# The first feed-forward's begun blocks: squares from token rows on ScalarE, the second input normalised on GpSimd, blocks begun in pairs, and an order of its own on each engine

## The chip, the cores and the metric

The kernel runs on one core of a Trainium2 chip. The core has a matrix engine (TensorE, in the profile PE), three engines for elementwise work (VectorE or DVE, ScalarE or ACT, GpSimd or POOL) and an engine that only issues transfers (SyncE or SP). Each engine works through a queue of its own in order; engines wait for each other by semaphores. The metric is the device time of one execution in microseconds (us), lower is better. Before the change it is 2115.48 us, the median of three runs.

## The reference

One encoder layer works on two inputs, `x_prompt` and `x_sample`, of 512 tokens by 1024 channels each. It is a half-step SwiGLU feed-forward, a mixing block (attention and an mLSTM side by side), a second half-step feed-forward and a last norm. Everything is float32. The change touches the first feed-forward:

```python
def rms_norm(x, g):
    y = xf * lax.rsqrt(jnp.mean(xf * xf, axis=-1, keepdims=True) + EPS)
    return (y * g.astype(jnp.float32)).astype(x.dtype)

def swiglu(x, w_gate, w_up, w_down):
    return (jax.nn.silu(x @ w_gate) * (x @ w_up)) @ w_down

x = x + 0.5 * swiglu(rms_norm(x, ffn1_norm), ffn1_w_gate, ffn1_w_up, ffn1_w_down)
```

`w_gate` and `w_up` are 1024 x 2816, that is 22 blocks of 128 columns each.

## The kernel before

**Products.** A float32 factor is split into a high part (ScalarE copies it into a shorter format) and a low part (VectorE subtracts the high part from it); `w_pair` does both for a weight block. A product is then three matmuls per 128 channels: high by high, high by low, low by high. `product` runs over 4 groups of 128 channels, so one product is 12 matmuls of 128 x 128 x 512.

**Seven products for eight.** The kernel treats the two inputs and the gate and up weights as a 2 x 2 block problem and multiplies it by a scheme with seven products (B11, B21, T2, T1, T3, B22, T4) in place of eight. The left factors are sums and differences of weight halves, the right factors `xc[...]` are sums and differences of the halves of the two normalised inputs (`x0l`, `x0u` of the first, `x1l`, `x1u` of the second). B11 and B21 need the first input only and give the first input's gate product: B11 is the lower half of its channels, B21 the upper half.

**Begun blocks.** Before the second input is ready TensorE can do B11 and B21 of a block. The kernel begins 12 of the 22 blocks in this way (`AHEAD[0]` is 12): for each, it evicts the sum after B11 (ScalarE, to SBUF), adds B21, takes the Silu of the whole, and stores both results in DRAM buffers `kept[j]`. Later, `up.rest` takes the blocks up again in the order 0, 12, 1, 13, ...: for begun blocks it loads `kept[j]`, for the others it does all seven products. The first product that isn't begun work is T2 of block 0; in the profile it is the first matmul group that writes `pss`.

**Raw blocks.** The norm's scale isn't known at the start. So the first six blocks (`RAW` is 6) multiply the raw input times the gain, split by `split_x`, and their results are multiplied by the scale `R[0]` afterwards (`raw_end`: two multiplies on VectorE, a Silu on ScalarE, two stores). Blocks 6 to 11 use the normalised input.

**The scale.** The inputs stand channel-major (`x_t`). `squares` squares 1024 columns at a time on ScalarE and adds them up on VectorE; `norm` adds the rest, sums over channels by transposes and a reduction (`col_sums`), takes the root in 11 small VectorE steps (`rstd_cols`), spreads the result over the partitions by transposes, and copies it to `R[s]`. `normed` multiplies the input by gain and scale, eight VectorE instructions of 512 columns for each input (L1247).

**What sets the order.** A scheduler orders the instructions of each engine, except where `pin` (`tc.keep_in_program_order`) keeps them as written. The matmuls of blocks, their weight loads (`up.left`) and the evictions of raw blocks aren't pinned. The weight loads go through four buffers (`wr`), the split weights through four others (`w8`). All loads and stores of this stretch are issued by SP, in SP's order; the small loads of the gains (`mix_gains`, L621 to L623) are issued by GpSimd.

```python
def raw_lower(j):                                  # L1251
    X = begun[j] = [PO() if j % 4 == 3 else MM(), held_rows[j % 4]]
    product(X[0], W[j][B11], xr[0], True)
    nc.scalar.activation(X[1], X[0], AF.Copy)
...
def raw_next(j):
    W.append(gu_left_a(raw2[0]) if j == 2 else up.left(j))
    raw_lower(j)
    raw_upper(j)

def ahead(j):
    W.append(up.left(j))
    up.begin(j, W[j])
```

Lines that the profile names: L249 and L250 are the high and low part of a weight block, L1229 and L1230 those of the raw input, L1282 and L1283 those of half an input (2048 columns), L290 is every matmul of `product`, L1254 the eviction of a raw block, L1234 and L1236 the squares and their sum, L1262 and L1263 the multiplies of `raw_end`, L1161 a square with its accumulator in a later stage, L892 and L1449 GpSimd's multiplies and adds in later stages.

Of the kernel before, what the change touches and what calls it, by code (L numbers as in the profile page):

```python
# [8 lines left out]
F32 = mybir.dt.float32  # L9
# [17 lines left out]
def encoder(ctx, tc, I, outs):  # L27
# [97 lines left out]
    nc.sync.dma_start(g1, I["ffn1_norm"])  # L125


# [5 lines left out]
    warm = cpool.tile([P, 1], F32, name="warm")  # L133
    nc.scalar.activation(warm, ones[:, 0:1], AF.Silu)
# [112 lines left out]

    def w_pair(t, src, pin=lambda i: i):
        pin(nc.scalar.activation(t[:, 0], src, AF.Copy))  # L249
        pin(V_.tensor_tensor(t[:, 1], src, f(t[:, 0]), op=ALU.subtract))  # L250
# [13 lines left out]
    def gu_left_b(rg, ru, ring, left):  # L264
# [5 lines left out]
        V_.tensor_tensor(a, u0, u1, op=ALU.add)  # L270
        V_.tensor_tensor(u0, g0, u0, op=ALU.subtract)
        V_.tensor_tensor(g0, a, g0, op=ALU.subtract)
        V_.tensor_tensor(g1_, g1_, g0, op=ALU.subtract)
        wb = w8_tile()
        w_pair(wb, halves(rg))
        left.update({T2_: part(wb, 0), B22: part(wb, 1)})

        def more():
            wd = [v(ring.wd(F32R)) for _ in range(2)]
            split(a, *wd)  # L280
            wc = w8_tile()
            w_pair(wc, halves(ru))
            left.update({T1: wd, T3: part(wc, 0), T4: part(wc, 1)})
# [95 lines left out]
    class Up:  # L379
# [33 lines left out]
        def rest(self, raw, at=None, hook=None):  # L413
            ring, ORDER = self.ring, self.order

            def resume(j):
                got = ring.v(), ring.h()
                for t, d in zip(got, self.kept.pop(j)):
                    nc.sync.dma_start(t[:, 0], d)
                return got  # L420

            left = {}
            gu_left_b(*raw, ring, left)()
            raw = self.fetch(ORDER[1])
            got = resume(ORDER[0])
# [192 lines left out]
    def mix_gains():  # L618
        pin = tc.keep_in_program_order
        for t, n in ((gm, "mix_norm"), (g2, "ffn2_norm")):  # L620
            pin(nc.gpsimd.dma_start(t, I[n][0].rearrange("(k p) -> p k", p=P)))  # L621
        pin(nc.gpsimd.dma_start(gbias, I["mlstm_gate_bias"].rearrange("a c -> (a c)").partition_broadcast(P)))
        pin(nc.gpsimd.dma_start(hn, I["mlstm_head_norm"][0].rearrange("(k p) -> p k", p=P)))  # L623
# [568 lines left out]
    def load_x(s, a, b):  # L1192
        nc.sync.dma_start(x_t[s][:, a:b, :], x_in[s][:, a:b, :])
# [3 lines left out]
    def load_half(j, a):  # L1197
        nc.sync.dma_start(half(first_w[j], a), half(up.v[0][j], a))

    load_half(0, 0)  # L1200
    load_x(0, 0, 1)
# [7 lines left out]
    raw2 = up.fetch(2, (0,))  # L1209
    for k in range(0, KD, 2):  # L1210
        load_x(1, k, k + 2)

    rings = up.ring
    stat = rings.x.rows[:3]
    held_rows = [t[:, i] for t in rings.x.rows[3:] for i in range(2)]
# [3 lines left out]
    W = [{}, {}]  # L1219

    def first_left(j, a):
        if a == 0:
            W[j]["t"] = w8_tile()
        w_pair(W[j]["t"][:, :, a], half(first_w[j], a))
        W[j][(B11, B21)[a]] = part(W[j]["t"], a)

    def split_x(k):
        t, kk, g, x = xr[k // HK_], k % HK_, g1[:, k:k + 1], x_t[0][:, k, :]
        nc.scalar.activation(t[:, 0, kk, :], x, AF.Copy, scale=g)  # L1229
        V_.scalar_tensor_tensor(t[:, 1, kk, :], x, g, f(t[:, 0, kk, :]), op0=ALU.mult, op1=ALU.subtract)  # L1230

    def squares(s, i):
        sq = stat[0] if i == 0 else stat[1 + i % 2]
        pin(nc.scalar.activation(sq, x_t[s][:, 2 * i:2 * i + 2, :], AF.Square))  # L1234
        if i:
            pin(V_.tensor_tensor(stat[0], stat[0], sq, op=ALU.add))  # L1236

    def norm(s):
        acc = stat[0][:, 0]
        pin(V_.tensor_tensor(acc, acc, stat[0][:, 1], op=ALU.add))  # L1240
        r = rstd_cols(col_sums(acc, pin=pin), 4, D, pin)
        pin(nc.scalar.activation(R[s], bcast_psum(r), AF.Copy))

    def normed(s):
        for k in range(KD):
            x = x_t[s][:, k, :]
            pin(V_.scalar_tensor_tensor(x, x, g1[:, k:k + 1], R[s], op0=ALU.mult, op1=ALU.mult))  # L1247
# [3 lines left out]
    def raw_lower(j):  # L1251
        X = begun[j] = [PO() if j % 4 == 3 else MM(), held_rows[j % 4]]
        product(X[0], W[j][B11], xr[0], True)
        nc.scalar.activation(X[1], X[0], AF.Copy)  # L1254

    def raw_upper(j):
        product(begun[j][0], W[j][B21], xr[1], False)

    def raw_end(j):
        X, v1 = begun.pop(j)  # L1260
        g0 = gate_rows()
        pin(V_.tensor_tensor(v1, v1, R[0], op=ALU.mult))  # L1262
        pin(V_.tensor_tensor(g0, X, R[0], op=ALU.mult))  # L1263
        pin(nc.scalar.activation(g0, g0, AF.Silu))
        up.kept[j] = kept[j]
        for t, d in zip((v1, g0), kept[j]):
            nc.sync.dma_start(d, t)

    def raw_next(j):
        W.append(gu_left_a(raw2[0]) if j == 2 else up.left(j))  # L1270
        raw_lower(j)
        raw_upper(j)

    def ahead(j):
        W.append(up.left(j))
        up.begin(j, W[j])
# [4 lines left out]
    def put_all(t, src):  # L1281
        pin(nc.scalar.activation(t[:, 0], src, AF.Copy))  # L1282
        pin(V_.tensor_tensor(t[:, 1], src, f(t[:, 0]), op=ALU.subtract))  # L1283
# [4 lines left out]
    raw_lower(0)  # L1288
    first_left(1, 0)
    first_left(0, 1)  # L1290
    for k in range(HK_, KD):
        split_x(k)
        if k % 2:
            squares(0, k // 2 - 2)
    raw_lower(1)
    raw_upper(0)
    first_left(1, 1)
    raw_upper(1)
    squares(0, 2)
    squares(0, 3)  # L1300
    norm(0)
    raw_next(2)
    raw_end(0)
    raw_end(1)
    raw_next(3)
    raw_end(2)
    normed(0)
    raw_next(4)
    raw_end(3)
    xc[B11], xc[B21] = xc_tile(), xc_tile()  # L1310
    for i, t in zip((B11, B21), halves(0)):
        put_all(xc[i], t)
    raw_next(5)
    raw_end(4)
    for i in range(4):
        squares(1, i)
    norm(1)
# [262 lines left out]
```

## Time and profile before

| | |
|---|---|
| median of 3 runs | 2115.48 us (2114.89 to 2115.61) |
| profiled execution: time, span | 2114.9 us, 2113.1 us |
| TensorE busy | 2067.0 us, 98% of the span |
| VectorE, ScalarE, GpSimd busy | 75%, 44%, 5% |
| granted TensorE clock, mean | 0.993 |
| memory traffic | 173 GB/s mean |

A profile row of an instruction group gives line, engine, operation, output<-inputs by the program's names with buffer numbers left out, size and count; then busy time and mean ns of one; then the engine's idle time just before the group and what ended it. A timeline row begins with the start and the length in us and ends with the idle time before it in brackets. A row of a stretch gives the window, its length, the busy us of PE, PEld (weight loading), DVE, ACT and POOL with their counts, the granted clock, the busy share of the 16 DMA engines and GB/s. A row of transfers gives the count, the KB of each and the median us from issue to landing.

### The profile page before, as it was taken

The page shows a single profiled execution, that of the slowest core. Times are in us where ns is not written, and L with a number is a line of the kernel's source. Part 1 is how long each engine was busy: PE and PEld are TensorE (multiplying, and loading weights), DVE is VectorE, ACT ScalarE, POOL GpSimd, SP SyncE. Part 2 cuts the span into 40 slices and gives each one's busy share as a digit, 9 for nine tenths or more (in the row PEclk, how much of TensorE's full clock was granted, in tenths as well). Part 3 has the DMA queues.
Part 4 walks back from the last instruction along what each step waited for, and adds up shares of the span by engine and source line. Part 5 has one row for each costly group of instructions (what it writes and reads, how often), then busy time and mean ns, then how long its engine had stood idle before and what let it go on. Part 6 is the DMA issues. An engine that isn't in the chain of part 4 may idle for free. (4 is left out here: it accounts for less than half of the span.)

```text
span 2113.1 us, 26149 instructions
## 1 busy us (share of the span) xinstructions
PE 2067.0 (98%) x9424; PEld 1689.1 (80%) x9424; DVE 1575.7 (75%) x2568; ACT 939.7 (44%) x1559; POOL 100.6 (5%) x105
## 2 busy tenths in 40 slices
PE   8899999999999999999999999999999999999997
PEld 6688888888888777878887787788788888888886
DVE  7978788786786796574649865764887877776687
ACT  6534344442225566463436555544543434343224
POOL 0000000001000110000101101010000000000002
PEclk9999999999999999999999999999999999999999
DMA  7445564699764222232341222344546544369753
GB/s 249 152 168 180 179 229 166 241 361 360 250 229 144 75 71 73 81 116 85 119 160 56 75 92 79 130 156 166 167 156 222 179 170 179 140 247 400 280 208 140
DMA packets 140625, 365.96 MB, mean 173 GB/s; under 512 B 13808, under 2 KB 13824, under 8 KB 139472
## 3 DMA queue, kind: packets, MB, share of 16 engines
q1 hardware_dynamic: 139648, 362.50, 48.4%
q0 software_dynamic: 560, 1.26, 0.2%
q8 instruction: 74, 1.21, 0.2%
q10 hardware_dynamic: 288, 0.52, 0.1%
q14 instruction: 55, 0.45, 0.1%
HBM read 258.82 MB, written 105.41 MB: 172 GB/s over the span
## 5 line engine op out<-in xcount | busy, mean ns | idle before, releaser
L290 PE MATMUL pss<-xc,w 128*128 128x512 f32 x1584 | 378.4, 390 | 0.7 <-DVE t L320 0.7
L290 PEld LDWEIGHTS pss<-xc,w 128*128 128x128 f32 x1584 | 297.3, 188 | 63.3 <-DVE t L320 1.4
L698 PE MATMUL mm<-xh,w 128*128 128x512 f32 x896 | 293.4, 397 | 0.9 <-DVE w L212 0.9
L290 PE MATMUL mm<-xc,w 128*128 128x512 f32 x1032 | 252.9, 397 | 18.0 <-DVE w L250 8.3
L249 ACT ACTIVATE w<-wr 128x1024 fp32r<-128x1024 f32 (+1 forms) x134 | 139.8, 1047 | 254.0 <-PE pst L290 134.3
L290 PEld LDWEIGHTS mm<-xc,w 128*128 128x128 f32 x1032 | 195.1, 191 | 64.0 <-DVE w L250 8.8
L250 DVE TENSOR_TENSOR w<-wr,w 128x1024 fp32r<-128x1024 f32 (+1 forms) x134 | 161.4, 1206 | 82.2 <-ACT w L249 81.5
L212 DVE TENSOR_TENSOR w<-wr,w 128x1024 fp32r<-128x1024 f32 (+1 forms) x112 | 135.4, 1210 | 116.2 <-ACT w L211 111.3
L698 PEld LDWEIGHTS mm<-xh,w 128*128 128x128 f32 x896 | 167.8, 189 | 33.4 <-DVE w L212 1.3
L542 PE MATMUL mm<-w,rt 128*128 128x512 f32 x792 | 185.3, 390 | 0.0
L698 PE MATMUL mm<-xl,w 128*128 128x512 f32 x448 | 177.4, 396 | 0.0
L542 PEld LDWEIGHTS mm<-w,rt 128*128 128x128 f32 x792 | 148.6, 188 | 30.7
L211 ACT ACTIVATE w<-wr 128x1024 fp32r<-128x1024 f32 (+1 forms) x112 | 114.6, 1030 | 109.8 <-PE pso L1127 35.0
L290 PE MATMUL pst<-xc,f 128*128 128x512 f32 x528 | 127.3, 390 | 0.0
L290 PE MATMUL pst<-xc,w 128*128 128x512 f32 x528 | 127.2, 390 | 0.0
L290 PEld LDWEIGHTS pst<-xc,w 128*128 128x128 f32 x528 | 99.0, 188 | 20.9 <-ACT t L323 0.5
L290 PEld LDWEIGHTS pst<-xc,f 128*128 128x128 f32 x528 | 99.2, 188 | 20.5
L602 ACT ACTIVATE w<-t 128x512 fp32r<-128x512 f32 x82 | 51.6, 632 | 121.9 <-PE pst L542 63.6
L602 ACT ACTIVATE w<-wr 128x512 fp32r<-128x512 f32 x72 | 44.7, 631 | 128.1 <-PE pso L542 62.0
L698 PEld LDWEIGHTS mm<-xl,w 128*128 128x128 f32 x448 | 84.6, 189 | 16.1
L542 PE MATMUL pss<-w,rt 128*128 128x512 f32 x396 | 94.4, 390 | 0.1
L542 PE MATMUL pst<-w,rt 128*128 128x512 f32 x396 | 94.0, 389 | 0.0
(344 smaller groups left out, 3506.2 us busy)
## 6 DMA issues: line engine op xcount, KB each, us to landing
rt<-rbuf SPq DMA_DIRECT2D x154, 512.0 KB, 6.0
rbuf<-t SPq DMA_DIRECT2D x72, 512.0 KB, 3.5
wr<-in_ffn_w_gate_dram SPq DMA_DIRECT2D x60, 512.0 KB, 4.2
wr<-in_w_in_cols_dram SPq DMA_DIRECT2D x56, 512.0 KB, 3.5
wr<-in_ffn_w_up_dram SPq DMA_DIRECT2D x44, 512.0 KB, 3.6
rbuf<-f SPq DMA_DIRECT2D x30, 512.0 KB, 3.8
rbuf<-tab SPq DMA_DIRECT2D x30, 512.0 KB, 3.8
wr<-in_ffn_w_down_dram SPq DMA_DIRECT2D x48, 256.0 KB, 7.0
```

What stands on the lines that cost most here:

```text
L211: pin(nc.scalar.activation(hi, raw, AF.Copy))
L212: pin(lo_eng.tensor_tensor(lo, raw, f(hi), op=ALU.subtract))
L249: pin(nc.scalar.activation(t[:, 0], src, AF.Copy))
L250: pin(V_.tensor_tensor(t[:, 1], src, f(t[:, 0]), op=ALU.subtract))
L290: nc.tensor.matmul(p, a[:, k, :], xt[:, b, k, :], start=(first and k == 0 and i == 0), stop=(k == HK_ - 1 and i == 2), skip_group_check=True)
L542: nc.tensor.matmul(p, r[:, b, d * P:(d + 1) * P], u[:, a, :], start=(first and q == 0 and k == 0), stop=(q == len(us) - 1 and k == 2), ski ...
L602: nc.scalar.activation(hi, src, AF.Copy)
L698: nc.tensor.matmul(p, a[:, k, :], b, start=(k == 0 and i == 0), stop=(k == n - 1 and i == 2))
```

## The change

The begun blocks of the first feed-forward are written anew; the rest of the kernel is as before.

- The token-major inputs are loaded too (`load_rows`, four loads of 512 KB for each input). `squares` squares a row block of 1024 columns on ScalarE in place and takes the sum of each token from the instruction's accumulator. The sums of squares on VectorE and `col_sums` are gone.
- The second input is multiplied by the gain on ScalarE (eight instructions) and by `R[1]` on GpSimd (eight instructions) in place of eight on VectorE.
- Blocks are begun in pairs: lower product of two blocks, then the upper products of both. Raw blocks use six banks of PSUM: three `MM`, one `PO` and the two `PS`.
- Nearly all of ScalarE's, VectorE's and SP's instructions of the stretch are pinned in the order written. `fetch_next` pins the load of a weight block on SP; blocks 2 to 7 are fetched ahead by name, blocks 8 to 11 by `left(j)` when their turn comes.
- The right factors T2, T1, T3, B22 and T4 are made after the last begun blocks in the written order, among the first block of `up.rest`.
- The first x load is issued by ScalarE, the gain `g1` after the first weights; the gains of later stages are laid out on the host so that each partition's values are contiguous.

```diff
+    def load_rows(s):
+        for b in range(4):
+            pin(nc.sync.dma_start(in_rows[:, b, :], xins[s][b * P:(b + 1) * P, :]))
+
+    def fetch_next(j):
+        raw = wpool.tile([P, KD, P], F32, tag="wr", bufs=4, name=nm("wr"))
+        pin(nc.sync.dma_start(raw, up.v[0][j]))
+        return raw
+
+    load_x(0, 0, 1, nc.scalar)
     load_half(0, 0)
-    load_x(0, 0, 1)
+    pin(nc.sync.dma_start(g1, I["ffn1_norm"]))
...
-    raw2 = up.fetch(2, (0,))
-    for k in range(0, KD, 2):
-        load_x(1, k, k + 2)
+    raws = {2: fetch_next(2)}
+    load_rows(0)
+    raws[3] = fetch_next(3)
...
+    def squares(s, b):
+        v = in_rows[:, b, :]
+        pin(nc.scalar.activation(v, v, AF.Square, accum_out=row_sq[s][:, b:b + 1]))
+
+    def root(s):
+        return rstd_cols(row_sq[s], 4, D, pin)
+
+    def spread(s, r):
         pin(nc.scalar.activation(R[s], bcast_psum(r), AF.Copy))
...
+    def left(j):
+        if j not in raws:
+            raws[j] = fetch_next(j)
+        W[j] = gu_left_a(raws.pop(j), pin)
...
+    def evac(j):
+        X, v1 = begun[j]
+        pin(nc.scalar.activation(v1, X, AF.Copy))
+        if j >= RAW:
+            nc.sync.dma_start(kept[j][0], v1)
...
+    def end(j):
         X, v1 = begun.pop(j)
-        g0 = gate_rows()
-        pin(V_.tensor_tensor(v1, v1, R[0], op=ALU.mult))
-        pin(V_.tensor_tensor(g0, X, R[0], op=ALU.mult))
-        pin(nc.scalar.activation(g0, g0, AF.Silu))
         up.kept[j] = kept[j]
-        for t, d in zip((v1, g0), kept[j]):
-            nc.sync.dma_start(d, t)
...
+        if j < RAW:
+            g0 = gate_rows()
+            pin(V_.tensor_tensor(g0, X, R[0], op=ALU.mult))
+            pin(V_.tensor_tensor(v1, v1, R[0], op=ALU.mult))
+            pin(nc.scalar.activation(g0, g0, AF.Silu))
+            nc.sync.dma_start(kept[j][0], v1)
+        else:
+            g0 = rings.k()
+            pin(nc.scalar.activation(g0, X, AF.Silu))
+        nc.sync.dma_start(kept[j][1], g0)
...
+    left(2)
+    squares(0, 0)
+    left(3)
+    squares(0, 1)
     squares(0, 2)
+    lower(2)
+    lower(3)
+    left(4)
+    evac(2)
     squares(0, 3)
...
+    evac(3)
+    r = root(0)
+    raws[5] = fetch_next(5)
+    raws[6] = fetch_next(6)
+    for k in range(0, KD, 2):
+        load_x(1, k, k + 2)
+    raws[7] = fetch_next(7)
+    load_rows(1)
+    left(5)
+    spread(0, r)
+    upper(2)
+    upper(3)
+    normed(range(4))
+    end(0)
+    hi_all(B11, x0l)
+    lower(4)
+    normed(range(4, 8))
+    lower(5)
+    evac(4)
+    hi_all(B21, x0u)
+    upper(4)
+    lo_all(B11, x0l)
+    lo_all(B21, x0u)
+    evac(5)
+    upper(5)
+    for k in range(KD):
+        x = x_t[1][:, k, :]
+        pin(nc.scalar.activation(x, x, AF.Copy, scale=g1[:, k:k + 1]))
+        if k == 1:
+            left(6)
+        if k == 3:
+            end(1)
+            squares(1, 0)
+        if k == 5:
+            left(7)
+            squares(1, 1)
+    end(2)
+    squares(1, 2)
+    lower(6)
+    squares(1, 3)
+    lower(7)
+    evac(6)
+    end(3)
+    upper(6)
+    r = root(1)
+    spread(1, r)
+    evac(7)
+    upper(7)
+    for k in range(KD):
+        x = x_t[1][:, k, :]
+        pin(G_.tensor_tensor(x, x, R[1], op=ALU.mult))
+    end(4)
+    end(6)
+    left(8)
+    end(5)
+    end(7)
+    left(9)
+    lower(8)
+    lower(9)
+    evac(8)
+    left(10)
+    upper(8)
+    evac(9)
+    upper(9)
...
+    pin(V_.tensor_tensor(x0l, x1l, x0l, op=ALU.subtract))
+    left(11)
+    end(8)
+    end(9)
+    raw0 = up.fetch(up.order[0])
...
+    lower(10)
+    lower(11)
+    evac(10)
+    hi_all(T1, x0l)
+    evac(11)
+    upper(10)
+    upper(11)
+    W0 = {}
+    more = gu_left_b(*raw0, rings, W0, pin)
+    lo_all(T1, x0l)
+    more()
```

191 lines of the change are left out of this document (82 added, 109 removed).

## The prediction

> **What bounds the kernel now.** I read the page's busy shares, then who waited for whom on TensorE, then TensorE's timeline of the first 110 us, then the stretches.
>
> ```profile
> PE 2067.0 (98%) x9424; PEld 1689.1 (80%) x9424; DVE 1575.7 (75%) x2568; ACT 939.7 (44%) x1559; POOL 100.6 (5%) x105
> ...
> PE mm L290 <- DVE w L250: 8.3, 1, 8.3
> PE mm L290 <- ACT xc L1229: 7.6, 1, 7.6
> ...
> 12.27 14.11 PE L290 MATMUL mm<-xc,w 128*128 128x512 f32 x48 [7.56 <-ACT xc L1229]
> 26.45 0.63 PE L184 MATMUL pst<-ident,t 128*128 128x128 f32 x4
> 48.68 10.06 PE L290 MATMUL mm<-xc,w 128*128 128x512 f32 x43 [1.16 <-ACT t L1254]
> 77.86 0.61 PE L290 MATMUL pst<-xc,f 128*128 128x512 f32 x2
> 89.68 4.20 PE L290 MATMUL mm<-xc,w 128*128 128x512 f32 x10 [8.35 <-DVE w L250]
> 93.71 1.08 PE L290 MATMUL pst<-xc,f 128*128 128x512 f32 x4
> 97.41 2.88 PE L290 MATMUL pss<-xc,w 128*128 128x512 f32 x12
> 104.67 2.88 PE L290 MATMUL pst<-xc,w 128*128 128x512 f32 x12
> 107.39 2.88 PE L290 MATMUL pss<-xc,w 128*128 128x512 f32 x12
> ```
>
> TensorE is busy 98% of the span, so only its idle time can be won or lost, and the two longest waits, 7.56 and 8.35 us, both lie in the stretch that the change rewrites. A full-speed group of 12 products takes 107.39 - 104.67 = 2.72, that is 0.227 each. The first 48 products end at 26.45. The row at 97.41 is product T2 of the first whole block; all 12 begun blocks lie before it, and also 6 products of T1 (the x2 and x4 rows). Without those 6, the same work stands at 97.41 - 6 x 0.227 = 96.05: this is my yardstick.
>
> ```profile
> 14.00:16.00 2.00, 2.00 (x6) 1.53 (x5) 2.00 (x4) 2.00 (x5) 0.00 (x0) 0.50 1.04 424
> 80.00:100.00 20.00, 11.65 (x44) 9.02 (x43) 19.39 (x20) 10.06 (x11) 0.00 (x0) 0.83 0.27 90
> 90.00:92.00 2.00, 2.00 (x6) 1.52 (x6) 2.00 (x3) 0.00 (x0) 0.00 (x0) 0.50 0.75 226
> 93.00:94.00 1.00, 1.00 (x6) 0.78 (x5) 0.95 (x3) 0.09 (x1) 0.00 (x0) 0.90 0.02 8
> ```
>
> In 80 to 100 VectorE (the third busy figure) works 19.39 of 20 us: it is late, and TensorE waits for it. Behind both waits the granted clock (the figure ahead of the DMA share) is 0.50; it is 0.90 in the mean of 93 to 94, so the second wait costs some 3.4 us of half speed besides.
>
> **What the change takes away.** Prices of one instruction:
>
> ```profile
> L1234 ACT ACTIVATE t<-xt 128x1024 f32<-128x1024 f32 x8 | 8.0, 1052 | 0.0
> L1254 ACT ACTIVATE t<-mm 128x512 f32<-128x512 f32 x5 | 3.0, 592 | 4.2 <-PE mm L290 4.2
> 22.92 2.95 ACT L249 ACTIVATE w<-wr 128x1024 fp32r<-128x1024 f32 x3
> 44.45 3.70 ACT L1282 ACTIVATE xc<-xt 128x2048 fp32r<-128x2048 f32 x2
> L1161 ACT ACTIVATION_READ_ACCUMULATOR f<-xs 128x1 f32 x24 | 4.5, 187 | 0.0
> L1236 DVE TENSOR_TENSOR t<-t,t 128x1024 f32<-128x1024 f32 x6 | 7.3, 1222 | 2.6 <-ACT t L1234 2.4
> L1247 DVE SCALAR_TENSOR_TENSOR xt<-xt,g,tab 128x512 f32<-128x512 f32 x8 | 5.4, 743 | 0.0
> L1262 DVE TENSOR_TENSOR t<-t,t 128x512 f32<-128x512 f32 x6 | 4.1, 684 | 1.4 <-ACT t L1242 1.4
> L1283 DVE TENSOR_TENSOR xc<-xt,xc 128x2048 fp32r<-128x2048 f32 x5 | 11.3, 2287 | 0.0
> 30.50 0.17 DVE L162 TENSOR_SCALAR rs<-rs 128x4 int32<-128x4 int32 x1
> 30.70 0.16 DVE L165 SCALAR_TENSOR_TENSOR rs<-rs 128x4 f32<-128x4 f32 x1
> ```
>
> VectorE loses the adds of squares, 6 x 1.22 = 7.3, and the eight multiplies of the second input, 5.4: 12.7 in all, more than the 8.35, and two column sums besides. So VectorE's lateness at 81 goes, and the wait of 8.35 with it. On ScalarE the eight squares stay eight instructions of 1024 columns; the accumulator's read (0.19, begun before the square ends) brings each to 1.05 from start to start. Eight scalings of 512 columns come on top, at no more than the 0.59 of an eviction (L1254): 4.4 in all, in ScalarE's queue ahead of weight splits. What is late next follows from the order in which the built program's instructions stand on each engine; I go through it with these prices (from start to start: a split of 1024 columns 0.95 on ScalarE and 1.14 on VectorE, a half of 2048 1.85 and 2.2, 512 columns 0.5 to 0.6).
>
> **First blocks.** Here the loads decide.
>
> ```profile
> 0.73 0.39 SPq L125 DMA_DIRECT2D g<-in_ffn_norm_dram  x1
> 1.17 0.42 SPq L1198 DMA_DIRECT2D wr<-in_ffn_w_gate_dram  x1
> 7.02 0.43 SPq L204 DMA_DIRECT2D wr<-in_ffn_w_gate_dram  x1
> wr<-in_ffn_w_gate_dram SPq DMA_DIRECT2D x1, 512.0 KB, 8.8
> q0 software_dynamic: 91, 0.01, 23.4%
> ```
>
> Weight block 2 landed at 7.02 + 8.8 = 15.8. Now the first weights go out 0.44 earlier, one x load leaves SP for ScalarE's queue (0.4), and GpSimd's gain loads, 23.4% of the DMA engines in 6 to 9, are gone: bounds 0.4 and 2, taken 1.4, so 14.4. All that the first 48 products need stands ahead of it; with at most 24 products left at that point they end by 14.4 + 24 x 0.227 = 19.8 (26.45 before). That takes the full clock: TensorE's first product starts with the first x load, not behind both weight halves, and no wait there is over 3 us; at half clock they would end by 25.2 and all that follows would come up to 2.4 later. But four loads of token rows now stand between weight blocks 2 and 3: 5 x 512 KB at 424 GB/s, 1.24 each, and block 3 lands at 20.6. ScalarE waits for it in order: split 21.7, two squares 23.8, split of block 4 24.8, eviction 25.3, last square 26.3; `root` on VectorE, 11 x 0.20, to 28.5. TensorE has done `lower(2)`, `lower(3)` (its low parts at 23.0) and four products of `upper(2)` at 26.2 and waits 2.4 for the broadcast. Then 68 products, 15.5, and the transposes: `upper(5)` ends at 44.7.
>
> Meanwhile ScalarE: R[0] 29.9; behind four multiplies and a `end(0)` step of VectorE the Silu at 33.9; halves of 1.85 and evictions to 39.9; four scalings and block 6's split 42.9; the Silu of `end(1)` 44.4 (VectorE: low halves 41.3, block 6 43.2); a square, two scalings, and block 7's split at 47.5. TensorE stands `lower(7)` first, so it waits 44.7 to 47.6 and 0.8 more for the low part: 3.7. `upper(6)` ends at 57.4, the second broadcast at 57.8, and behind R[1] and `evac(7)`, in order on ScalarE, `upper(7)` ends at 61.9. Both gaps hang on the landing of block 3, one to one. The 1.16 that TensorE waited for an eviction at 48.68 is gone, with two more banks; the chain above has no wait there.
>
> **Blocks 8 to 11.** Here lies the price. Weight loads 8 to 11 are not fetched ahead: in SP's order load 8 stands behind the store of block 6's Silu, load 9 behind block 7's Silu, loads 10 and 11 behind the stores of `evac(8)` and `evac(9)`. SP waits at each store for ScalarE, and the load queued behind it waits too, though its buffer has long been free. ScalarE in turn waits for the load with the next Silu or eviction queued behind the split: a ring of four turns.
>
> ```profile
> wr<-in_ffn_w_gate_dram SPq DMA_DIRECT2D x5, 512.0 KB, 4.1
> DMA to landing us min/median/max: 3.9/4.3/4.7
> DMA to landing us min/median/max: 2.0/3.4/3.9
> 60.60 0.32 SPq L408 DMA_DIRECT2D kept<-f  x1
> ```
>
> The first row is the weight loads at 40 to 100; the second those at 40 to 70, the third the 256 KB stores and loads of `kept` there. A store's issue and its signal take 0.45. Load 8: the Silu of `end(6)`, which needs `upper(6)` and stands behind R[1], is done at 60.0, landing 60.5 + 4.1 = 64.6, split 65.7; TensorE has waited since 61.9: 3.8. The low part takes VectorE 1.2 and perhaps GpSimd's share (below, 0.65), 67.6, so 1.5 more. Load 9 hangs on that: `end(5)` 68.2, two Silus 69.4, landing 74.0, split 75.1; `lower(8)` ended at 70.1, so TensorE waits 5.0, then 1.5 for the low part, and ends `lower(9)` at 79.4. Load 10: `evac(8)` 75.6, landing 80.2, split 81.2. Load 11: 81.7, 86.3, 87.4, low part 88.7. Then VectorE alone: two differences and two low halves, 4 x 1.14, 93.4; six sums 3.6, 97.0; split 98.1 and low 99.3. TensorE is through `upper(11)` at 98.2 (it waited there for evictions behind the same chain), and T2 starts as if unbroken at 99.4. VectorE then owes 7.9 (two whole halves 4.4, two weight parts 2.3, two small ops 1.2) to 107.2, against 28 products to 105.8: 1.6, and 0.3 later. The trace of before has no such wait; between 0 and 3.8 I take 1.9.
>
> **GpSimd's eight multiplies.**
>
> ```profile
> L892 POOL TENSOR_TENSOR box<-box,tab x32: 1266/1294/2278, 705.4 to 1316.0; 128x512 f32<-128x512 f32 x32
> 2060.52 5.14 POOL L1449 TENSOR_TENSOR xs<-xs,tab 128x512 f32<-128x512 f32 x3
> 2062.75 3.47 DVE L603 TENSOR_TENSOR w<-wr,w 128x512 fp32r<-128x512 f32 x2
> 2066.14 0.68 DVE L603 TENSOR_TENSOR w<-t,w 128x512 fp32r<-128x512 f32 x1
> ```
>
> Alone one takes 1.29; while three ran in 5.14, two VectorE adds of 0.68 took 3.47. From 58.5 eight take 10.3 to 15, done by 74, before VectorE needs them at 83: off the path. VectorE pays up to 1.3 for each two-input op meanwhile; two are on the chain, and I take half: 0.65 each. The Trainium skill, SBUF — State Buffer, "Who interferes with whom", says that such a VectorE op and a GpSimd op block each other for a whole instruction; the rows agree, and by the full block the sum would be 1.3 more.
>
> **At nothing.** The gains laid out on the host: their first reader stands behind the first feed-forward, so their loads may wait behind the eight multiplies. The warm-up Silu moved behind one DMA issue on ScalarE: hidden by the first landing. The 4 MB of token rows beyond those counted: 5 us of DMA between 30 and 40, when TensorE has all its weights.
>
> **Sum.** 99.4 + 1.9 - 96.05 = 5.2 later; nothing behind it is reordered on TensorE. The profiled run took 2114.9 (span 2113.1 and 1.8 around it), 0.6 under the median 2115.48: 2120.1 on its own time, 2120.7 as a median.
>
> **Rivals.** Every us of landing counts four times.
> *Short landings*: the stretch at 60 to 90 moves little else, and the four loads land faster. At 2.8 the sum is nil; at the 2.0 of the fastest `kept` transfer it is 5.2 - 8.4 = -3.2: 2112.3. For it: the queue is nearly empty at 60 to 90. Against it: no weight load there was under 3.9. By the Trainium skill, DMA: Bandwidth & Descriptors, "Anatomy of one DMA" (about 2 us and the bytes at 436 GB/s), a landing would be 3.2 and the time 2117.1, no measurable change; the 4.1 row disagrees.
> *VectorE late*: the full block on GpSimd (1.3), landings of 4.7 (2.4) and a doubled debt behind T2 (1.9) give 2126.3. For it: 19.39 of 20 in the row at 80. Decides if low parts of blocks 8 and 9 take over 2.
> *Clock*: the waits of 3.8 and 5.0 could halve the clock, as the one of 8.35 did (row at 90). Fifteen products at half speed lose 15 x 0.227 = 3.4. TensorE's own work would end at 79.4 + 6 x 2.72 = 95.7, and T2 starts at 99.4 for VectorE's chain: it hides there. The sum stays, and no chance is set aside.
>
> **Numbers.** Forecast 0.55, short landings 0.27, VectorE late 0.18. 0.2% is 4.2 us, about what a measurement can tell from none. Faster by more needs landings of 1.75 or block 3 landing 3 us sooner as well: 0.12. Within it: 0.15 of the short landings, 0.16 of the forecast's low part: 0.31. Slower: 0.57. The range goes from 2111.5 (2112.3, and 0.8 for the first loads) to 2126.5.
>
> **What would show it.** Right: the first 48 products end near 20, a 2 us gap before the first broadcast, one of 3 to 4 near 45, gaps of 4 and 5 before blocks 8 and 9 laid to ACT w and behind it DMA wr, and no 8 us gap. Wrong: loads 8 and 9 landing before TensorE is through block 7, or T2 before 96.

## The result: 0.34% slower, and the profile after

The changed kernel takes 2122.87 us in the median of seven runs (2121.41 to 2123.58), the kernel before 2115.48 on the same chip, in seven runs too (2114.36 to 2117.03); the ratio is 1.0034, with a 95% interval of 1.0022 to 1.0046. The forecast was 2120.7 and "slower" the likeliest. The profiled run took 2121.88 with a span of 2120.1, which is 7.0 over the span before.

From the changed kernel's page the busy shares, and from its waits on TensorE (total, times, longest) the two largest:

```profile
PE 2069.4 (98%) x9416; PEld 1687.4 (80%) x9416; DVE 1559.2 (74%) x2550; ACT 944.6 (45%) x1575; POOL 110.0 (5%) x113
...
PE mm L289 <- ACT w L248: 7.9, 2, 4.8
PE pso L289 <- ACT w L248: 5.6, 1, 5.6
```

TensorE's timeline, with start, duration, instruction, and in brackets the idle time just before it and what ended it:

```profile
8.83 12.35 PE L289 MATMUL mm<-xc,w 128*128 128x512 f32 x53 [0.28 <-DVE xc L1244]
27.74 0.62 PE L189 MATMUL pst<-ident,rs 128*128 128x128 f32 x4 [2.08 <-DVE rs L168]
46.97 5.47 PE L289 MATMUL mm<-xc,w 128*128 128x512 f32 x11 [3.15 <-ACT w L248]
68.76 1.22 PE L289 MATMUL mm<-xc,w 128*128 128x512 f32 x2 [4.77 <-ACT w L248]
80.00 5.05 PE L289 MATMUL pso<-xc,w 128*128 128x512 f32 x12 [5.59 <-ACT w L248]
102.49 0.73 PE L289 MATMUL pss<-xc,w 128*128 128x512 f32 x2
```

The waits of 7.56 and 8.35 us are gone. The first 48 products are the 7 before 8.83 and 41 of the 53 in that row: they end at 18.1 to 18.4 (26.45 before). At 27.74 the new kernel is still ahead. Then come three waits for weight splits (ACT w), of 3.15, 4.77 and 5.59, and T2 starts at 102.49 instead of the yardstick's 96.05: 6.4 later, of the 7.0 in all.

The stretches (busy time of TensorE, weight loads, VectorE, ScalarE and GpSimd; granted clock; DMA share) show the same from the other side. VectorE was busy for 19.39 of 20 us at 80 to 100. In the changed kernel it has little to do at 60 to 80 (3.19 of 20 us), and TensorE too is busy for 8.41 us only:

```profile
60.00:80.00 20.00, 8.41 (x25) 5.66 (x25) 3.19 (x4) 5.18 (x9) 13.39 (x13) 0.76 0.41 133
80.00:100.00 20.00, 19.01 (x74) 14.80 (x75) 12.84 (x12) 8.91 (x11) 0.00 (x0) 0.90 0.70 248
```

Who makes them wait is read from ScalarE's timeline, and why the loads are late from SP's below it (SPq: a DMA's issue):

```profile
67.65 1.06 ACT L248 ACTIVATE w<-wr 128x1024 fp32r<-128x1024 f32 x1 [5.76 <-DMA wr<-in_ffn_w_gate_dram]
78.89 1.06 ACT L248 ACTIVATE w<-wr 128x1024 fp32r<-128x1024 f32 x1 [6.92 <-DMA wr<-in_ffn_w_gate_dram]
84.62 1.06 ACT L248 ACTIVATE w<-wr 128x1024 fp32r<-128x1024 f32 x1 [4.19 <-DMA wr<-in_ffn_w_gate_dram]
90.67 1.06 ACT L248 ACTIVATE w<-wr 128x1024 fp32r<-128x1024 f32 x1 [4.50 <-DMA wr<-in_ffn_w_gate_dram]
```

```profile
61.92 1.97 SPq L1297 DMA_DIRECT2D kept<-f  x1
63.94 0.43 SPq L1208 DMA_DIRECT2D wr<-in_ffn_w_gate_dram  x1
73.27 0.43 SPq L1208 DMA_DIRECT2D wr<-in_ffn_w_gate_dram  x1
80.83 0.42 SPq L1208 DMA_DIRECT2D wr<-in_ffn_w_gate_dram  x1
86.57 0.42 SPq L1208 DMA_DIRECT2D wr<-in_ffn_w_gate_dram  x1
```

Each load of blocks 8 to 11 is issued (63.94, 73.27, 80.83, 86.57) only after the split of the block before it (none, 67.65, 78.89, 84.62), and each split waits for its load. The loads take 3.7, 5.6, 3.8 and 4.1 us from issue to the start of the split.

### The profile page after: what moved, and what is told of

Same layout as the page of the kernel before. It is cut to its first block, busy times and chain, and to the rows that moved or that the text cites. A ratio compares the mean times of both kernels' runs of the same rounds, so it can differ in the third digit from the quotient of the medians.

```text
span 2120.1 us, 26131 instructions
## 1 busy us (share of the span) xinstructions
PE 2069.4 (98%) x9416; PEld 1687.4 (80%) x9416; DVE 1559.2 (74%) x2550; ACT 944.6 (45%) x1575; POOL 110.0 (5%) x113
## 4 chain that ended last, share of the span: by engine, by line
PE 86%; DVE 6%; ACT 4%; DMA 2%; issue 1%; SPq 0%; POOL 0%; ACTq 0%; DVEq 0%; POOLq 0%
PE pss L289 17%; PE mm L698 14%; PE pst L289 11%; PE mm L289 8%; PE mm L542 8%; PE pst L542 4%; PE pss L542 4%; PE mm L682 4%; PE mm L1127 3%; PE pso L542 3%; PE pso L954 2%; PE pso L682 1%; DMA wr<-in_ffn_w_gate_dram 1%; PE pss L926 1%; PE pso L1083 1%
## 5 line engine op out<-in xcount | busy, mean ns | idle before, releaser
L289 PE MATMUL pss<-xc,w 128*128 128x512 f32 x1632 | 389.8, 389 | 0.2 <-DVE w L249 0.2
L289 PEld LDWEIGHTS pss<-xc,w 128*128 128x128 f32 x1632 | 306.2, 188 | 64.8 <-DVE w L249 0.6
L289 PE MATMUL mm<-xc,w 128*128 128x512 f32 x936 | 231.8, 397 | 13.9 <-ACT w L248 7.9
L289 PEld LDWEIGHTS mm<-xc,w 128*128 128x128 f32 x936 | 176.9, 191 | 57.6 <-ACT w L248 8.8
L289 PEld LDWEIGHTS pst<-xc,w 128*128 128x128 f32 x528 | 99.0, 188 | 20.9 <-DVE xc L1307 0.2
```

Source lines behind the costliest of these rows:

```text
L289: nc.tensor.matmul(p, a[:, k, :], xt[:, b, k, :], start=(first and k == 0 and i == 0), stop=(k == HK_ - 1 and i == 2), skip_group_check=True)
```

## The experiments

All start from the changed kernel, and the ratios are to the kernel before on the same chip, each with its 95% interval. The kernel before takes 2112.4 to 2115.5 us in the median from chip to chip, so the ratios compare kernels better than the spans do. T2 and the span are those of the profiled run.

| kernel | ratio | T2 | span |
|---|---|---|---|
| before | 1 | 97.41 (yardstick 96.05) | 2113.1 |
| changed | 1.0034 (1.0022 to 1.0046) | 102.49 | 2120.1 |
| loads 8 to 11 early | 0.9967 (0.9955 to 0.9979) | 88.08 | 2106.2 |
| multiplies on VectorE | 1.0034 (1.0021 to 1.0047) | 100.39 | 2118.6 |
| block 3's load first | 1.0035 (1.0023 to 1.0047) | 101.06 | 2120.1 |
| block 6 before 7 | 1.0050 (1.0038 to 1.0062) | 103.49 | 2122.6 |
| loads early, blocks 6 and 7 early | 0.9967 (0.9955 to 0.9979) | 86.30 | 2103.1 |
| loads early, block 3's first | 0.9966 (0.9953 to 0.9978) | 86.43 | 2104.8 |
| loads early, multiplies on VectorE | 0.9983 (0.9974 to 0.9992) | 90.24 | 2106.6 |
| gain loads first | 1.0047 (1.0034 to 1.0060) | 101.12 | 2121.1 |
| all of the early edits | 0.9965 (0.9952 to 0.9977) | 86.11 | 2104.7 |
| waits before 8 and 9 filled | 1.0043 (1.0029 to 1.0057) | 103.53 | 2125.3 |
| loads 8 and 9 early | 0.9997 (0.9988 to 1.0006) | 93.50 | 2112.1 |
| wait before 7 filled | 1.0046 (1.0032 to 1.0059) | 100.46 | 2117.5 |

An interval's half width is some 2.5 us, and from T2 to the end of the span the kernels take between 2016.4 us (2106.6 - 90.24, multiplies on VectorE with early loads) and 2021.8 (2125.3 - 103.53, waits before 8 and 9 filled), with the same work. Where these 5 us lie I did not settle; some of it is chance between executions, for the profiled run of the second was 4.1 us above that kernel's other four. T2 scatters too. The changed kernel, block 6 before 7 and the two filled kernels have the same code up to the end of block 5, and TensorE is through it at 43.8, 44.3, 45.8 and 43.8 us. So a shift of T2 by 2 us or less between two traces isn't by itself shown to come from the edit, and one under 3 us doesn't show in a time. Where an edit does less than that, what follows goes by the stretch that it touches.

**The loads early.** The part undone is the loads' place in SP's order.

```
     load_rows(1)
+    raws[8] = fetch_next(8)
     left(5)
+    raws[9] = fetch_next(9)
...
             left(6)
+            raws[10] = fetch_next(10)
...
             left(7)
+            raws[11] = fetch_next(11)
```

> The changed kernel with the weight loads 8 to 11 issued ahead of the stores: load 8 right behind the second token rows, 9 behind block 5's split, 10 and 11 behind the splits of blocks 6 and 7. Nothing else moves. Theory one (the waits of 4.77 and 5.59 us before blocks 8 and 9 are the loads' place in SyncE's order): both waits fall below 2.7 us, together below 4; T2, the first product of the first whole block, comes at 88 to 92 instead of 102.5, and the own time is 8 to 13 us shorter, 2107 to 2112, faster than the kernel before too. Rival (VectorE has a debt that the waits cover): T2 comes at 90 but TensorE then waits for VectorE behind it, and the time is within 4 us of the changed kernel. Rival (the loads were not the cause, ScalarE's and VectorE's order is): T2 stays above 99.

TensorE's timeline of this kernel:

```profile
49.72 0.82 PE L289 MATMUL mm<-xc,w 128*128 128x512 f32 x2 [3.15 <-ACT w L248]
62.59 5.79 PE L289 MATMUL mm<-xc,w 128*128 128x512 f32 x24 [1.18 <-ACT f L1278]
68.51 0.73 PE L289 MATMUL pso<-xc,w 128*128 128x512 f32 x2
76.94 11.25 PE L289 MATMUL mm<-xc,w 128*128 128x512 f32 x48
88.08 0.73 PE L289 MATMUL pss<-xc,w 128*128 128x512 f32 x2
```

From 62.59 to T2 there is no wait that the timeline names: the 24 products there are block 7's upper and block 8's lower half, back to back. T2 is 14.4 earlier and the span 13.9 shorter, somewhat more than theory one gave (8 to 13); the time falls below the kernel before by 0.33%, 0.67% below the changed kernel's ratio. Both rivals fall: nothing is given back behind T2 that the scatter would let one see, and the orders of ScalarE and VectorE, which were left as they were, are fast enough for T2 at 88.

**Loads 8 and 9 alone.** Are all four loads links of the chain, or only the two whose waits TensorE shows? The edit is shown against the kernel with all four early.

```
-            raws[10] = fetch_next(10)
-            raws[11] = fetch_next(11)
```

> The changed kernel with the weight loads 8 and 9 alone early; 10 and 11 are left behind the stores. Theory (each load stands behind the store that the block before it frees, so two early ones put the rest ahead as well, and loads 10 and 11 then land before TensorE is through block 9): T2 within 1 of 88.1, the time within 1 of the kernel with all four early, 2106.2 by the profiled span. Rival (all four stand in the chain, and each left behind costs its wait): a wait of 2 to 5 us before block 10 or 11, T2 at 90 to 95, and the time 2 to 7 longer than with all four early.

ScalarE and TensorE of this kernel:

```profile
72.75 1.06 ACT L248 ACTIVATE w<-wr 128x1024 fp32r<-128x1024 f32 x1 [4.36 <-DMA wr<-in_ffn_w_gate_dram]
81.68 1.06 ACT L248 ACTIVATE w<-wr 128x1024 fp32r<-128x1024 f32 x1 [7.39 <-DMA wr<-in_ffn_w_gate_dram]
```

```profile
82.79 0.73 PE L289 MATMUL mm<-xc,w 128*128 128x512 f32 x2 [3.15 <-ACT w L248]
93.50 0.73 PE L289 MATMUL pss<-xc,w 128*128 128x512 f32 x2
```

The rival holds in its numbers: load 10 costs TensorE nothing, but load 11, issued at 74.68 behind the store of block 9's eviction, is split only at 81.68, 7.0 later, and TensorE waits 3.15 before block 11. T2 lies 5.4 behind that of four early loads, and the time, at 0.9997, is that of the kernel before. But not all of this is load 11's place in the order. It took 4.1 in the changed kernel; here GpSimd issues its four gain loads at 73.9 to 76.2, beside it. Had it landed in 4.1, its split would have begun at 78.8, before TensorE was through the products that stand ahead of block 11, at 79.6. So load 11 is a link here together with the gain loads, and what its place alone costs isn't shown. That the changed kernel's timeline shows no wait before block 11 did not mean that this load was free: TensorE was late itself.

**The clock.** The prediction let the half clock hide behind the chain. Products that nobody reads, into the bank that the block's first product overwrites, keep TensorE busy in its waits before blocks 8 and 9:

```
+    def fill(j, n):
+        for i in range(n):
+            pin(nc.tensor.matmul(begun[j][0], x[:, 0, i % HK_, 0:P], x[:, 0, i % HK_, :], start=True, stop=True, ...))
...
-    lower(8)
-    lower(9)
+    lower(8, 20)
+    lower(9, 34)
```

> The changed kernel with products that nobody reads in TensorE's waits before blocks 8 and 9, 20 and 34 of them into the bank that the block's first product then overwrites; the loads stay late. It asks what of the loss is the clock. Theory (block 8's slow products are hidden, since the split of block 9 comes no sooner; block 9's are not, since TensorE runs on from there to T2): the granted clock of 60 to 90 stays at 1, lower 8 and lower 9 take 2.9 each instead of 5.4 and 5.05, and T2 and the time come 1.8 to 2.6 earlier. Rival (both slow stretches are hidden, as the prediction's 3.4 us were): T2 and the time within 0.7. Rival (both count): 4 to 5 earlier.

TensorE's timeline:

```profile
64.82 4.69 PE L1271 MATMUL mm<-xc 128*128 128x512 f32 x20
71.41 2.60 PE L289 MATMUL mm<-xc,w 128*128 128x512 f32 x10 [0.94 <-DVE w L249]
81.56 3.20 PE L289 MATMUL pso<-xc,w 128*128 128x512 f32 x12
103.53 0.73 PE L289 MATMUL pss<-xc,w 128*128 128x512 f32 x2
```

Ten products of block 8 take 2.60 where the changed kernel's took 4.13, and block 9's twelve 3.20 where they took 5.05. T2 moves all the same only with load 8, which is issued at 64.90 here: from there to T2 it is 38.63 us, and 38.55 in the changed kernel. My theory (block 9's half counts) is wrong, and the first rival, the prediction's own step, is right: both slow stretches lie hidden behind the loads. The ratio, 1.0043, isn't below the changed kernel's 1.0034 either.

The wait of 3.15 before block 7 lies ahead of load 8, so its clock was tried by itself, with 12 such products and block 7 held ahead of block 6:

```
-    lower(6)
+    lower(7, 12)
     squares(1, 3)
-    lower(7)
+    lower(6)
```

> The changed kernel with twelve products that nobody reads in TensorE's wait of 3.15 us before block 7, into the bank that the block's first product then overwrites; block 7's lower half is held ahead of block 6's, as the changed kernel's planner has it, and the loads stay late. It asks whether the clock that halves behind that wait delays load 8, the first of the chain. Theory (it does: block 7's and 6's lower halves then take 2.7 each instead of 5.5 and 3.4, the eviction of block 6, for which ScalarE waits 3.88, comes 2 to 3 earlier, and load 8 and the whole chain with it): from the first eviction of block 5 to load 8's issue 1.5 to 3 less than the changed kernel's 25.5 (38.42 to 63.94), and T2 and the time 1.5 to 3 earlier. Rival (ScalarE's squares or block 3's held bank set the eviction of block 6): load 8 and T2 within 0.7.

TensorE's timeline:

```profile
43.77 2.88 PE L1271 MATMUL mm<-xc 128*128 128x512 f32 x12
48.35 2.56 PE L289 MATMUL mm<-xc,w 128*128 128x512 f32 x10 [0.53 <-DVE w L249]
100.46 0.73 PE L289 MATMUL pss<-xc,w 128*128 128x512 f32 x2
```

From the eviction of block 5 (38.53) to that of block 6 (53.67) it takes 15.1 us, and 17.2 in the changed kernel. In eight other kernels with the same order there it takes 15.9 to 16.5. So this clock is on the path up to block 6's eviction, but its price is 0.8 to 2.1 us, and the changed kernel's profiled run shows the most of it. At load 8 the gain can't be told from other things: from block 5's eviction to load 8's issue (61.84) it takes 23.3 us instead of 25.5, but also 22.7 to 23.1 in three kernels without a filled wait, in which no store is issued as slowly as in these two (1.97 in the changed kernel, 2.13 here, 0.3 to 0.4 in those three). T2 is 2.0 earlier, no more than the scatter, and the times show nothing: the profiled run is the fastest of five, and the ratio, 1.0046, is not below the changed kernel's.

**Block 6 before block 7.** Why does TensorE wait for block 7's weights at 43.8 when block 6's are split at 42.5? I took it for a poor choice of the scheduler and held the products in the program's order.

```
-        product(begun[j][0], W[j][B11], (xr[0] if j < RAW else xc[B11]), True)
+        product(begun[j][0], W[j][B11], (xr[0] if j < RAW else xc[B11]), True, *([pin] if j in (6, 7) else []))
```

> The changed kernel with the products of the lower halves of blocks 6 and 7 held in the order of the program on TensorE: block 6, whose weights are split at 42.5, before block 7, split at 47. Theory (the planner's order is what makes TensorE idle for 3.15 us and lose its clock): TensorE goes on at 43.8 without a wait over 1 us, the granted clock of 46 to 52 stays at 1, upper half of block 6 ends about 3 us earlier, load 8 is issued about 2.5 earlier since it stands behind block 6's store, and T2 and the time come 2 to 3 earlier. Rival (load 8 and what follows it set the end, whatever comes before): the 3.15 wait goes but the wait before block 8 grows by as much, T2 within 0.7 of 102.5, the time the same.

TensorE's timeline:

```profile
50.61 4.49 PE L289 MATMUL pso<-xc,w 128*128 128x512 f32 x12 [6.30 <-DVE t L1290]
```

The theory falls, and so does its rival: the wait doubles to 6.30 and has another cause. Block 6's bank (`pso`) still holds block 3, which VectorE reads in `end(3)`, at 49.8. Block 7's bank was free, which fits the order that the scheduler had chosen.

**GpSimd's part.** The eight multiplies on VectorE instead, behind the end of block 6:

```
-        pin(G_.tensor_tensor(x, x, R[1], op=ALU.mult))
...
     end(6)
+    for k in range(KD):
+        x = x_t[1][:, k, :]
+        pin(V_.tensor_tensor(x, x, R[1], op=ALU.mult))
     left(8)
```

> The changed kernel with the eight multiplies of the second input by its root row on VectorE instead of GpSimd, placed behind the end of block 6; GpSimd then issues its four gain loads at the start. Theory (GpSimd's work held up SyncE's issue of 1.97 us and VectorE's steps at 68 to 72, and its gain loads stretched load 9's landing to 5.6): the store's issue takes 0.4 again, load 8 is split at 66.1 instead of 67.65, load 9 lands in about 4.1, T2 comes 3 to 4.5 earlier and the time is 3 to 4 shorter, near 2118.5. Rival (GpSimd costs nothing, the long issue and landing are chance): T2 within 0.7 of 102.5 and the time the same. Rival (VectorE's 5 us of multiplies come back as a debt behind T2): T2 earlier, the time the same or up to 2 us longer.

This moves the four gain loads to the start as well, so those were moved by themselves too:

```
+    mix_gains()
     first_left(0, 0)
...
-    tail = up.rest(raw0, 13, mix_gains, W0)
+    tail = up.rest(raw0, 13, lambda: None, W0)
```

> The changed kernel with GpSimd's four gain loads issued at the start, ahead of the multiplies, as the kernel before has them. Theory (they stretched the landing of load 9 from 4.1 to 5.6, since they are issued at 71 to 74 while load 9 is under way): load 9's landing is 4.0 to 4.4, the wait of 5.59 before block 9 falls to about 4.2, T2 and the time come 1.2 to 1.6 earlier. Rival (the multiplies on GpSimd hold the landing up, which ended at 71, or chance does): landing still above 5.2 and the time the same. Where the multiplies' cost to VectorE is what the experiment with them on VectorE showed, there remain 0.5 to 0.8 us between this kernel's T2 and that one's 100.4.

With the gain loads first, load 9 is issued at 73.66 and split at 77.52, 3.9 instead of 5.6; with the multiplies on VectorE it is 4.2. In four more kernels that issue the gain loads late it is 5.4 to 5.7. So the gain loads stretch that landing by some 1.5 us. T2 comes 1.4 and 2.1 earlier, less than the 3 to 4.5 that the first theory gave; what the multiplies themselves cost is at most the 0.7 between the two, and not shown. The store's issue of 1.97 us was not theirs: where they are on GpSimd as before (gain loads first, block 3's load first) it takes 0.33. But load 8 gains only 0.4 by it, since most of what it saves in issue it loses in landing: from that store's issue to the split it is 5.7 us in the changed kernel, and 5.3 in these two (62.30 to 67.58, 60.12 to 65.42) and with the multiplies on VectorE (62.28 to 67.62). The times show none of these shifts.

The same swap on top of the early loads:

> The kernel with the weight loads 8 to 11 early, and the eight multiplies of the second input on VectorE instead of GpSimd, behind the end of block 6. Theory (with the loads early VectorE is busy from 60 on, so its relief is worth something only now): the 5 us of multiplies delay the low part of block 8 by up to 2.5 us and the halves of the whole block behind it, T2 comes 1 to 4 later than 88.1 or TensorE waits for VectorE behind it, and the time is 1 to 5 longer than with the early loads alone. Rival (GpSimd's 16 us of multiplies beside a busy VectorE cost VectorE as much as they relieve it): the time within 1 us of it. Rival (GpSimd is the slower way): the time 1 to 3 shorter.

VectorE's timeline with the multiplies on VectorE, and below it with them on GpSimd, both with the loads early:

```profile
62.12 4.91 DVE L1397 TENSOR_TENSOR xt<-xt,tab 128x512 f32<-128x512 f32 x8 [3.90 <-ACT tab L1254]
73.58 2.28 DVE L1411 TENSOR_TENSOR xt<-xt,xt 128x2048 f32<-128x2048 f32 x1
```

```profile
71.87 3.37 DVE L1411 TENSOR_TENSOR xt<-xt,xt 128x2048 f32<-128x2048 f32 x1
75.16 2.31 DVE L249 TENSOR_TENSOR w<-wr,w 128x1024 fp32r<-128x1024 f32 x1
```

Here the theory holds in the trace: TensorE waits 2.12 us for block 8's low part, which stands behind the multiplies, and had no such wait with them on GpSimd. T2 comes 2.2 later, and the ratio rises from 0.9967 to 0.9983, of intervals that just overlap. GpSimd's help is no gift: beside it the 2048 columns take 3.37 instead of 2.28, and block 11's low part 2.31 where 1.23 is usual. That agrees with the Trainium skill, SBUF — State Buffer, "Who interferes with whom": a VectorE instruction with two inputs in SBUF contends with a GpSimd instruction that reads SBUF.

**Block 3's load first.**

```
     raws = {2: fetch_next(2)}
-    load_rows(0)
     raws[3] = fetch_next(3)
+    load_rows(0)
```

> The changed kernel with the load of weight block 3 issued ahead of the four first token-row loads instead of behind them. Theory (all stages up to T2 hang on one chain, so an early wait that goes shortens the whole): block 3 is split near 17 instead of 19.8, the waits of 0.52 before block 3's low part and of 2.08 before the first broadcast shrink by 1.5 to 2.6 together, and T2 and the time come 1.5 to 2.6 earlier. Rival (each early wait is taken up by the next one, block 7's and load 8's): the first broadcast comes earlier but T2 stays within 0.5 of 102.5 and the time is the same. Rival (the rows then land late): the root is not earlier, and nothing moves.

On top of the early loads:

> The kernel with the weight loads 8 to 11 early, and weight block 3's load ahead of the first token rows. Theory (with the loads off the path the chain from the first broadcast to T2 is unbroken, so what an early wait loses reaches T2): first broadcast about 1 to 1.5 earlier, T2 at 86.5 to 87, the time 1 to 1.5 shorter than with the early loads alone. Rival (ScalarE's order at block 7 or VectorE behind T2 takes it up): T2 within 0.5 of 88.1 or the time the same.

The split of block 3 moves from 19.80 to 17.70, the first broadcast from 27.74 to 26.76, and T2 from 102.49 to 101.06; with the early loads T2 moves from 88.08 to 86.43. That is the size of the theories, but the edit isn't shown to be the cause. Both shifts are within the scatter of T2, and with the early loads the first broadcast comes only 0.4 earlier (28.51 for 28.90). The rest lies behind it, where the clock was half at 30 to 32 with the early loads alone (0.50) and full in this kernel; the shorter wait before it (0.38 for 2.03) may have saved that. The ratios (1.0035, 0.9966) do not move.

**A better version.** Block 7's split right behind block 6's, and blocks 2 and 3 ended earlier, so that both weights and bank are there (the lines are taken out where they stood before, and the early loads are left out here):

```
         if k == 1:
             left(6)
+            left(7)
         if k == 3:
             end(1)
+            end(2)
+            end(3)
...
+    lower(7)
+    lower(6)
+    evac(6)
     squares(1, 2)
     squares(1, 3)
```

> The kernel with the weight loads 8 to 11 early, and besides: block 7's split right behind block 6's, the ends of blocks 2 and 3 right behind block 1's (so that VectorE frees block 3's bank, which block 6 takes, some 4 us earlier), and the evictions of blocks 6 and 7 ahead of two of the squares. Theory (the waits of 3.15 and 0.44 before block 7 and the slow products behind them come from ScalarE's order and, for block 6, from the held bank): TensorE goes on from block 5 to 7 without a wait over 1 us, the granted clock of 40 to 60 is 1, T2 comes at 82 to 85 instead of 88.1, and the time is 3 to 6 us shorter than with the early loads alone, 2100 to 2104 on the scale of 2106.2. Rival (VectorE is now late: behind T2 it has to catch up): T2 at 84, but waits for VectorE's low parts behind it grow by as much and the time is the same within 1.5 us. Rival (ScalarE's queue holds the upper halves instead): T2 above 87.

TensorE then has no wait before block 7. But it has one of 2.62 for the eviction of block 6, which stands in ScalarE's queue behind two squares and four scalings, and T2 comes at 86.30, 1.8 earlier: between the theory and its last rival. The ratio stays. The next version takes all the early edits together, with that eviction ahead of three squares:

```
         if k == 5:
+            lower(7)
+            lower(6)
+            evac(6)
+    squares(1, 1)
+    evac(7)
...
+    upper(7)
+    left(8)
     r = root(1)
```

> Candidate that should beat both kernels: the weight loads 8 to 11 early, block 3's load ahead of the first token rows, block 7's split right behind block 6's, the ends of blocks 2 and 3 behind block 1's, the evictions of blocks 6 and 7 ahead of the later squares, and block 8's split ahead of the ends of blocks 4 and 6. Theory (what is left before T2 are ScalarE's places in its queue: 2.62 us before block 6's upper half, 1.24 and 0.99 before block 8): T2 comes at 82 to 84.5 instead of 86.3 (blocks 6 and 7 early without these) and the time is 1.5 to 4 shorter than that kernel's, a ratio to the kernel before of 0.994 to 0.996. Rival (VectorE, whose busy share is 0.94 to 0.99 from 80 to 120, sets the end): T2 earlier but TensorE waits for it behind T2, and the ratio stays at 0.9966.

The theory's 82 to 84.5 is missed: the waits before block 6's upper half and in block 8 are down to 0.69 and 0.53, but one of 3.17 now comes before block 9, and T2 comes at 86.11. Its time, 0.9965, is that of the early loads alone. Each of the three versions that add early edits to the early loads shows a T2 some 2 us earlier, which is within its scatter, and gives nothing that the times could tell; the version with the early loads is the one to keep: it beats the kernel before by 0.33% and the changed kernel by 0.67%.

## Why the prediction was right, and where its steps were off

The direction, the place and the mechanism were right: VectorE is relieved, the two long waits go, and a ring of four loads behind SP's stores costs more than they did. The size was 2.2 us short (2120.7 for 2122.87). Of the two terms of the sum, T2 was off by more, and the other hid part of it.

**VectorE and the first blocks**: right. The 8.35 wait is gone; the first 48 products end at 18.1 to 18.4 (forecast 19.8); the clock before 20 us is 1; block 3's split is done at 20.9 (21.7); the broadcast waits 2.08 (2.4). But the reason given for the full clock, no wait over 3 us, doesn't carry it: the kernel with blocks 6 and 7 early has the same code there and no wait over 1.3 us, and its clock was 0.50 at 10 to 14. That it was 1 here is in part luck.

**Block 7**: the wait was right (3.15, forecast 2.9 and 0.8 more), the step behind it was not. I had named a clock risk only for the waits of 3.8 and 5.0, and had counted block 7's products at full speed. Two rows of the changed kernel's stretches (TensorE's busy time, clock, DMA share, GB/s):

```profile
42.00:47.00 5.00, 1.85 (x10) 0.94 0.29 108
47.00:51.00 4.00, 3.96 (x9) 0.50 0.20 74
```

Behind the wait of 3.15 the clock is half: 11 products take 5.47 instead of 2.5. Against the filled kernel this puts block 6's eviction, and load 8 behind it, 2.1 us later (0.8 to 1.4 in the other kernels). It is in no term of my sum.

**The ring**: right in form, four turns; the terms were too small. Load 8 was issued at 63.94 for a forecast of 60.5: some 2 for that clock, and 1.6 for the store ahead of it, whose issue took 1.97 where I counted 0.4. From that store's issue to the split I counted 4.6 (0.45 and 4.1); it took 5.3 to 5.7 in the six kernels in which three stores are issued within 1 us just before it. So block 8's split began at 67.65 (64.6). Load 9 took 5.6, of which the gain loads were 1.5: I had laid them "at nothing", since their reader comes late, and had not asked what else was landing when they went out at 71. Loads 10 and 11, at 3.8 and 4.1, were as forecast. All this put the end of load 11's split at 91.73 (87.4). From there the chain to T2 was 1.2 shorter than forecast (10.8 for 12.0), so that T2 came at 102.49 (99.4).

**Block 8's and 9's clock**: right. It fell to half behind both waits (0.50 at 69 to 72, 0.51 at 80 to 84), and it is hidden.

**VectorE's debt** behind T2, 1.9: not there in the profiled pair. From T2, counted from the yardstick, to the end it was 2113.1 - 96.05 = 2017.05 before and 2120.1 - 102.49 = 2017.6 after: 0.6. The scatter of that quantity over the kernels, 5 us, is larger than the term, so no run settles it. T2 was 3.1 too early in the forecast and the debt 1.3 too large; that they are of opposite sign is luck, and made the sum look better than it was.

**The rivals**: *Short landings* did not occur, the shortest was 3.7. The section of the Trainium skill behind the 3.2 in that rival (DMA: Bandwidth & Descriptors, "Anatomy of one DMA") gives its fit for transfers that GpSimd issues; these loads are SP's, and all four landings, 3.7 to 5.6, lie above it. *VectorE late* asked for low parts of over 2 us at blocks 8 and 9; they took 1.48 and 1.22. GpSimd's eight multiplies took 10.88 (10.3 to 15). *Clock* named the waits before blocks 8 and 9, which are the hidden ones, and not the one before block 7.

## What to carry to other kernels

A load that needs nothing but a free buffer does not belong behind stores that wait for the engine it feeds: in one in-order queue that makes a ring, and each of its turns costs a landing; here the four loads were worth 14 us, twice what the whole change lost. Look for that ring in the issue times of the loads against the instructions that they feed, not in TensorE's waits alone: these showed two of the four loads, and a third became a wait once the first two were out of the way. And ask of anything that is "off the path" what else is under way when it runs.

## What the hardware did that I had not expected

- Behind a wait of 3.15 us TensorE's clock was half (stretch 47 to 51: 0.50); behind one of 2.62, with blocks 6 and 7 early, it stayed at 1. In that same kernel it was half behind two waits of 1.24 and 0.99 with two products between them, by these stretches:

```profile
53.00:57.00 4.00, 3.66 (x16) 1.00 0.25 94
60.00:61.00 1.00, 0.04 (x1) 1.00 0.38 135
62.00:63.00 1.00, 0.31 (x1) 0.89 0.34 129
63.00:64.00 1.00, 1.00 (x3) 0.50 0.37 74
```

  The wait of 2.08 before the first broadcast went both ways: the first row is the changed kernel's, the second that of the kernel with the waits before 8 and 9 filled, which has the same code there.

```profile
30.00:32.00 2.00, 2.00 (x10) 1.00 1.05 414
30.00:32.00 2.00, 2.00 (x6) 0.50 1.06 416
```

  So the length of a wait doesn't settle by itself what the clock does. The Trainium skill, TensorE: Matmul & The Clock Gate, "Why this matters for your kernels", asks for no idle gap over some 3 us. The first two waits agree with it; the pair, 2.2 us idle in two pieces, and the wait of 2.08 in the filled kernel do not.
- Four gain loads of 2 to 8 KB on GpSimd's queue stretched the landing of a 512 KB weight load that was under way from 3.9 to 5.6 us (and load 11, with loads 8 and 9 early, took 7.0 beside them for 4.1 in the changed kernel; three more weight loads were issued right behind it there and in the changed kernel alike).
- GpSimd and VectorE slow each other: eight multiplies of 512 columns took 10.88 us on GpSimd beside a mostly idle VectorE and 16.48 beside a busy one, which itself lost 1.1 on some of its larger steps (3.37 for 2.28, 2.31 for 1.23).
